# A routed layer's output rows: written with the residual on a token's first visit, added to on its second

## The chip, the cores and the metric

The kernel runs on one core of one Trainium2 chip. The metric is the device time of one execution in microseconds (us). Of the core's engines, TensorE (PE) multiplies, VectorE (DVE) and ScalarE (ACT) work on tiles, GpSimd (POOL) issues the transfers that go through lists of row numbers, and SyncE (SP) issues the other transfers; 16 DMA engines carry them out.

## The reference, cut to what matters

A decoder layer: attention and a recurrence make the residual stream `x`; then 1024 tokens go through a routed feed-forward block of 32 experts in 4 groups, each token to two experts of one group.

```python
h2 = rms_norm(x, norm2_g) * (1.0 + scale2) + shift2
x = x + gate2 * hierarchical_moe(h2, ...)
...
g_p, g_idx = lax.top_k(g_prob, 1)
e_p, e_idx = lax.top_k(jax.nn.softmax(e_logits, axis=-1), TOP_K)   # TOP_K = 2
expert = g_idx * EXPERTS_PER_GROUP + e_idx
...
hid = jax.nn.silu(xb @ w_gate[e]) * (xb @ w_up[e])
return hid @ w_down[e]
...
y = jnp.zeros((N + 1, D), jnp.float32).at[row_tok].add(y_rows)[:N]
```

## The kernel before, in words

The first 500 us compute the mixers and, tile by tile of 128 tokens, the residual row `x1`, its norm factor `ivx`, the router and the places of the tokens in their experts' lists. `h2_rows` writes each tile of `x1` to `out` (L1238, on POOL's queue) and `h2 = x1 * ivx` to `h2_d` in HBM (L1247, on SP's queue). `places` builds, by products of one-hot matrices, a table `tb` of token numbers and gate weights for all experts.

The experts then run as 20 units (`UNITS`). A unit is a block of 128 rows, filled by one expert or by up to four experts of different groups, in multiples of 32 rows. The two experts of a token never share a unit. Units 0 to 4 hold eight "front" experts (two of each group) whose weights are loaded early; the other 24 experts are ranked by their counts, and `overflow_tables` builds the lists of what runs over an expert's first 128 rows. For unit n:

- `gather` (L1437, POOL): an indirect DMA brings the unit's rows of `h2_d` into a buffer `xe`, of which there are `NXE` (two). A list entry outside the 1024 tokens is skipped.
- `xpose` (L1610, PE): eight transposes into `pxe`; ACT and DVE copy them out as `xeT` (L1614, L1616).
- `gate_up` (L1649, PE): products with the expert's gate and up weights into `pgu`; `act` (L1623, L1625) forms `hid`; `hid_t` (L1632, L1634) transposes it.
- `down` (L1660, PE): products with the down weights into `py`; DVE multiplies by the row `g2` into `y` (L1663); an indirect DMA adds the rows of `y` to the rows of `out` (L1665, POOL, a scatter).

The weights of an expert are six blocks of 512 KB, loaded by SP into the pool of 128x1024 blocks (`blk`, `NBLK` of them); a load waits for the fourth load before it (`fly`, L1125), so four are in flight. The loop calls `step` three times per unit; each takes one piece of `tables()` and puts it on DVE and PE between the unit's own work. A scheduler sets the final order on each engine. Transfers that touch the same tensor are ordered by semaphores: each scatter waits until the scatter before it has landed.

Of the kernel before, what the change touches and what calls it, by code (L numbers as in the profile page):

```python
# [20 lines left out]
D = 1024  # L21
S = 1024
# [20 lines left out]
ROWS = [("gqp", 64), ("gkp", 64), ("freq", 32), ("br", 36)]  # L43
# [52 lines left out]
MULTI = [u for u in UNITS if len(u) > 1]  # L96
NFU = 5
GRP = [("same", 32), ("in", 4), ("by", 4), ("base", 1), ("full", 32), ("shift", 32)]
GOFF = {}
_o = 0  # L100
for _n, _w in GRP:
# [37 lines left out]
def layer(ctx, tc, A, out, dbg=None, stop=None):  # L139
# [193 lines left out]
    V.tensor_scalar(tokm, tokc[:, :NT], -float(S), None, op0=OP.add)  # L333
# [840 lines left out]
    NXE = 2  # L1174
# [26 lines left out]
    rec = c2.tile([128, NT, 2, 2], F32, name="rec")  # L1201
    tb = c2.tile([128, 64], F32, name="tb")
# [32 lines left out]
    def h2_rows(t):  # L1235
        x1 = St[t]["x"]
        tsl = slice(t * 128, t * 128 + 128)
        G.dma_start(out[tsl, :], x1)  # L1238
        h2 = blk("h2")
        iv = ivx[:, t:t + 1]  # L1240
        if OPT["h2p"][t] == "S":
            SC.activation(h2, x1, AF.Copy, scale=iv)
        elif OPT["h2p"][t] == "V":
            V.tensor_scalar(h2, x1, iv, None, op0=OP.mult)
        else:
            G.tensor_mul(h2, x1, iv.to_broadcast([128, D]))
# [194 lines left out]
    def column(p, m):  # L1441
        if p < NF:
            e = FRONT[p]
            return tk0[:, e:e + 1], tb[:, 32 + e:33 + e]
        if m:
            c = EBASE[p] + m - 1
            return toi[:, c:c + 1], tow[:, c:c + 1]
        return tki[:, p:p + 1], tkw[:, p:p + 1]

    def plan(u):  # L1450
        if len(u) == 1:
            i, w = column(*u[0][:2])
        else:
            c = MULTI.index(u)
            i, w = pki[:, c:c + 1], pkw[:, c:c + 1]
        n = max(g[2] + g[3] for g in u) * 32
        return i[:n], w[:n], [(0, i[:n])]

    pki = c2.tile([128, len(MULTI)], I32, name="pki")
    pkw = c2.tile([128, len(MULTI)], F32, name="pkw")  # L1460
    xrow = {0: gather(plan(UNITS[0])[0])}

    def pack(pieces):
        for c, (p, m, a, n, r) in pieces:
            i, w = column(p, m)
            V.tensor_copy(pki[32 * a:32 * (a + n), c:c + 1], i[r:r + 32 * n])
            last["pack"] = V.tensor_copy(pkw[32 * a:32 * (a + n), c:c + 1], w[r:r + 32 * n]).ins

    def pieces(us, late):
        return [(MULTI.index(u), g) for u in us if len(u) > 1 for g in u if bool(g[1]) == late]  # L1470
# [30 lines left out]
    pT = bank("pT")  # L1501
    for c in range(2):
        T.transpose(pT[:32, c * 128:c * 128 + 128], tb[:, c * 32:c * 32 + 32], ident)
    tT = half("tT")[:32, :256]
    V.tensor_copy(tT, pT[:32, :256])
    pS_ = bank("psort")
    for c in range(2):
        T.matmul(pS_[:, c * 32:c * 32 + 32], tT[:, c * 128:c * 128 + 128], R, start=True, stop=True)
    tki = c2.tile([128, 32], I32, name="tki")
    V.tensor_scalar(tki, pS_[:, :32], trash, None, op0=OP.add)  # L1510
    tkw = c2.tile([128, 32], F32, name="tkw")
    V.tensor_copy(tkw, pS_[:, 32:64])
    tow = c2.tile([128, NOV], F32, name="tow")
    toi = c2.tile([128, NOV], I32, name="toi")
    pack(pieces(UNITS[2:NFU], False))
# [3 lines left out]
    def overflow_tables():  # L1519
# [47 lines left out]
        V.tensor_scalar(si, si, 7, None, op0=OP.logical_shift_right)  # L1567
# [4 lines left out]
        V.scalar_tensor_tensor(rec[:, :, :, 0], pf, -1.0, tokm[:, :, None].to_broadcast(SH), op0=OP.mult, op1=OP.add)  # L1572
        yield
        pto = bank("pto")[:, :2 * NOV]
        for c in range(2):
            for t0 in range(0, NT, 4):
                ts = slice(t0, t0 + 4)
                oh = t3(half("ov"), 4)
                V.tensor_tensor(oh, iota[:, None, :].to_broadcast([128, 4, 128]),
                                pf[:, ts, c:c + 1].to_broadcast([128, 4, 128]), op=OP.is_equal)  # L1580
                ob = half("ov")
                bo = t3(ob[:, 8 * NOV:12 * NOV], 4)
                V.tensor_tensor(bo, iota[:, None, :NOV].to_broadcast([128, 4, NOV]),
                                ext[:, ts, c:c + 1].to_broadcast([128, 4, NOV]), op=OP.is_equal)
                rh = ob[:, :8 * NOV].rearrange("p (t a e) -> p t a e", t=4, a=2)
                V.tensor_tensor(rh, bo[:, :, None, :].to_broadcast([128, 4, 2, NOV]),
                                rec[:, ts, c, :, None].to_broadcast([128, 4, 2, NOV]), op=OP.mult)
                for t in range(4):
                    T.matmul(pto, oh[:, t], rh[:, t].rearrange("p a e -> p (a e)"), start=(t0 + t == 0 and c == 0),
                             stop=(t0 + t == NT - 1 and c == 1))  # L1590
# [184 lines left out]
```

## Time and profile before

| | |
|---|---|
| median of 3 runs | 815.01 us (810.57 to 818.53) |
| the profiled execution | 816.49 us |
| its span, first to last instruction | 814.6 us |
| mean granted clock of PE | 0.971 of full |
| busy: PE, DVE, ACT, POOL | 728.1, 447.2, 317.0, 157.6 us |
| HBM read, written | 160.61 MB, 22.95 MB |

The span is some 500 us of mixers, norm and router, then the units. Busy times overlap; a share of the whole span hides that each stretch has a limit of its own. "Landing" of a transfer is the time from the start of the instruction that issues it until its data has arrived.

### The profile page before, as it was taken

Reading aid. Unit: us, or ns where it says so; the run is one execution under the profiler, and the core shown is the slowest. Engines: PE = TensorE matmul, PEld = TensorE weight load, DVE = VectorE, ACT = ScalarE, POOL = GpSimd, SP = SyncE. Lnnn points to the kernel's source line nnn. Section 1 sums busy time; section 2 is a strip of 40 time slices with the busy share of each in tenths; the row PEclk is TensorE's granted clock in tenths of the full one; section 3 lists DMA queues with packets and bytes.
Section 4 is the critical chain, followed back from the end, with each engine's and each line's share of the span. In section 5 each row is a group of like instructions: output and inputs, shape, how many; then the busy total and the mean of one; then the engine's idle time right before and its main releaser. Section 6 shows DMA issues by size and latency. Waiting matters only on the chain. (4 is left out here: it accounts for less than half of the span.)

```text
span 814.6 us, 12260 instructions
## 1 busy us (share of the span) xinstructions
PE 728.1 (89%) x4257; PEld 471.2 (58%) x4257; DVE 447.2 (55%) x1334; ACT 317.0 (39%) x715; POOL 157.6 (19%) x150
## 2 busy tenths in 40 slices
PE   3899999989988989899999997699979899999874
PEld 1477776548877878788888886333333343332321
DVE  4597386868777469797884667344334222213210
ACT  3455456666354157667664434121201211102200
POOL 1121012103665102031311000212112112212010
PEclk9989999999999999999999998699989999999998
DMA  9952437681317403020154789999999999999994
GB/s 311 372 151 84 143 108 236 210 280 58 109 44 259 168 39 104 1 79 1 54 173 144 259 311 343 346 316 349 313 373 330 329 335 336 369 347 354 304 320 102
DMA packets 70976, 180.47 MB, mean 222 GB/s; under 512 B 8960, under 2 KB 22528, under 8 KB 70912
## 3 DMA queue, kind: packets, MB, share of 16 engines
q1 hardware_dynamic: 63328, 158.50, 55.1%
q0 software_dynamic: 7104, 21.00, 9.5%
q8 instruction: 34, 0.56, 0.3%
q10 hardware_dynamic: 480, 0.16, 0.2%
q14 instruction: 30, 0.25, 0.1%
HBM read 160.61 MB, written 22.95 MB: 225 GB/s over the span
## 5 line engine op out<-in xcount | busy, mean ns | idle before, releaser
L1649 PE MATMUL pgu<-ew,xeT 128*32 128x512 f32 (+1 forms) x928 | 163.4, 613 | 8.1 <-DMA ew<-in_w_e 7.3
L1649 PEld LDWEIGHTS pgu<-ew,xeT 128*32 128x32 f32 (+1 forms) x928 | 48.3, 121 | 99.4 <-issue 79.0
L1660 PE MATMUL py<-ew,hT 128*32 128x512 f32 (+1 forms) x464 | 75.1, 597 | 5.8 <-ACT hT L1634 5.8
L225 PE MATMUL pp<-hTh,winh 128*128 128x512 f32 x176 | 69.2, 406 | 5.8 <-DVE hTh L188 3.0
L226 PE MATMUL pp<-hTl,winh 128*128 128x512 f32 x176 | 71.1, 404 | 0.0
L227 PE MATMUL pp<-hTh,winl 128*128 128x512 f32 x176 | 70.4, 401 | 0.0
L1663 DVE TENSOR_TENSOR y<-py,m_g 128x512 f32<-128x512 f32 (+1 forms) x40 | 27.5, 691 | 69.3 <-PE py L1660 64.3
L1623 ACT ACTIVATE sg<-pgu 128x256 f32<-128x256 f32 (+1 forms) x20 | 7.7, 387 | 142.9 <-PE pgu L1649 135.8
L1660 PEld LDWEIGHTS py<-ew,hT 128*32 128x32 f32 (+1 forms) x464 | 23.5, 120 | 48.3 <-issue 35.7
L1616 DVE TENSOR_SCALAR xeT<-pxe,gc,mc 128x128 f32<-128x128 f32 x80 | 27.4, 404 | 33.0 <-PE pxe L1610 33.0
L225 PEld LDWEIGHTS pp<-hTh,winh 128*128 128x128 f32 x176 | 34.0, 194 | 16.3 <-DVE hTh L188 4.0
L1665 POOL DMA_INDIRECT out<-y,pki x13 | 20.7, 1589 | 111.2 <-DVE y L1663 87.7
L1625 DVE SCALAR_TENSOR_TENSOR hid<-sg,pkw,pgu 128x256 f32<-128x256 f32 (+1 forms) x13 | 6.2, 479 | 63.4 <-ACT sg L1623 60.9
L1634 ACT ACTIVATE hT<-pht 128x256 f32<-128x256 f32 (+1 forms) x20 | 7.6, 380 | 85.1 <-PE pht L1632 65.4
L1614 ACT ACTIVATE xeT<-pxe,mc,gc 128x128 f32<-128x128 f32 x80 | 30.0, 461 | 24.9 <-PE pxe L1610 24.9
L226 PEld LDWEIGHTS pp<-hTl,winh 128*128 128x128 f32 x176 | 33.9, 193 | 9.9 <-issue 2.1
L227 PEld LDWEIGHTS pp<-hTh,winl 128*128 128x128 f32 x176 | 34.1, 194 | 8.6 <-issue 1.7
L949 ACT ACTIVATE P<-pS,nb,scq 128x384 f32<-128x384 f32 (+2 forms) x48 | 32.3, 679 | 12.2 <-DVE nb L946 12.2
L983 PE MATMUL po<-PT,v 128*128 128x256 f32 (+1 forms) x160 | 35.8, 362 | 0.0
L1046 POOL TENSOR_TENSOR wo<-wo,m_g 128x256 f32<-128x256 f32 x32 | 28.2, 916 | 15.3 <-DMA wo<-in_w_out 15.3
L983 PEld LDWEIGHTS po<-PT,v 128*128 128x128 f32 x160 | 28.8, 191 | 2.9
L1610 PEld LDWEIGHTS pxe<-ident,xe 128*128 128x128 f32 x160 | 18.2, 145 | 20.7 <-issue 14.4
(424 smaller groups left out, 1613.6 us busy)
## 6 DMA issues: line engine op xcount, KB each, us to landing
ew<-in_w_e SPq DMA_DIRECT2D x186, 512.0 KB
wad<-in_w_ada SPq DMA_DIRECT2D x64, 256.0 KB
wada<-in_w_ada SPq DMA_DIRECT2D x16, 512.0 KB
win<-in_w_in SPq DMA_DIRECT2D x12, 512.0 KB
xt<-in_x SPq DMA_DIRECT2D x8, 512.0 KB
wo<-in_w_out SPq DMA_DIRECT2D x8, 512.0 KB
xr<-in_x SPq DMA_DIRECT2D x8, 512.0 KB
x_d<-xr SPq DMA_DIRECT2D x8, 512.0 KB
```

Of the source, the lines that this page charges most:

```text
L225: T.matmul(o, lhi, rhi, start=first, stop=False)
L226: T.matmul(o, lhi, rlo, start=False, stop=False)
L227: T.matmul(o, llo, rhi, start=False, stop=last)
L949: SC.activation(Pt[:, o:o + w], pss[ci], AF.Exp, scale=P["scq"][:, i:i + 1], bias=nb, accum_out=l[:, ci:ci + 1])
L983: T.matmul(po[:, o:], P["v"][:, js], PT[j // 4][:, j % 4, o:], start=(j == 0), stop=(j == nj - 1), skip_group_check=True)
L1046: EN[OPT["g1"]].tensor_mul(w[:, q:q + 256], w[:, q:q + 256], mrow["g1"][:, q:q + 256])
L1614: SC.activation(xT[a][:, c], pt[:, c], AF.Identity, scale=gc[:, k:k + 1], bias=sh2[:, k:k + 1])
L1616: last["dve"] = V.tensor_scalar(xT[a][:, c], pt[:, c], gc[:, k:k + 1], sh2[:, k:k + 1], op0=OP.mult, op1=OP.add).ins
L1649: T.matmul(pg[r], xT[k // 4][:, c + r.start:c + r.stop], w[k // 2][:, NS[k % 2]], start=(k == 0), stop=(k == 7), skip_group_check=True)
L1660: T.matmul(py[n][r], hT[:, a * 128 + r.start:a * 128 + r.stop], w[4 + a][:, NS[n]], start=(a == 0), stop=(a == 1), skip_group_check=True)
L1663: last["dve"] = V.tensor_mul(y[:rows, NS[n]], py[n][:rows], mrow["g2"][:rows, NS[n]]).ins
L1665: G.indirect_dma_start(out=out, out_offset=bass.IndirectOffsetOnAxis(ap=idx, axis=0), in_=y[r0:r0 + idx.shape[0]], in_offset=None, compute ...
```

## The change

`h2_rows` no longer writes `x1` to `out`. The tables carry a third value per row: `1/ivx` where the row is the token's first visit in the order of the units, 0 where it is the second. `down` forms `x * r + y` in the gathered buffer (`x` is `h2`, so `h2/ivx = x1`) and sends it to `out` by two indirect DMAs in place of one: first the add, with the list of second visits, then a plain write, with the list of first visits; each list has an entry outside the tokens in the rows of the other. Unit 0 has no add. There are three `xe` buffers and 40 blocks. `tb` holds the front experts alone; the tables of all others are built by one pass (`late_tables`), of which a `step` takes three pieces.

```diff
-NBLK = 41
+NBLK = 40
-NX = 2
+NX = 3
...
+ONCE = {}
+for _n, _u in reversed(list(enumerate(UNITS))):
+    for _g in _u:
+        if _g[0] < NF:
+            ONCE[FRONT[_g[0]] // GE] = _g[0]
...
     def h2_rows(t):
...
-        G.dma_start(out[tsl, :], x1)
...
     def places(g):
...
+        inc = sm.tile([128, 2, 32], F32, name="inc", bufs=1)
+        V.tensor_tensor(inc, pp3, RW("cff")[:, None, :].to_broadcast([128, 2, 32]), op=OP.is_lt)
+        V.tensor_mul(scr, inc[:, :, None, :].to_broadcast([128, 2, 2, 32]), M[:, ts])
+        fst = two(2, "fst")
+        V.tensor_reduce(fst, scr, op=OP.add, axis=AX.X)
+        V.reciprocal(rinv[:, ts], ivx[:, ts])
+        V.tensor_mul(fst, fst, rinv[:, ts, None].to_broadcast([128, 2, 2]))
+        for c in range(2):
+            V.tensor_sub(rec[:, ts, c, 2], rinv[:, ts], fst[:, :, 1 - c])
...
+    def lists(c0, c1, src=None, dst=None):
+        v = pk[:, c0:c1] if src is None else src
+        get, put, add, t = dst or [x[:, c0:c1] for x in (idx["get"], idx["put"], idx["add"], fsh)]
+        V.tensor_scalar(get, v[:, :, 0], float(OOB), None, op0=OP.add)
+        V.tensor_scalar(t, v[:, :, 2], 0.0, 2.0 * OOB, op0=OP.is_gt, op1=OP.mult)
+        V.scalar_tensor_tensor(put, v[:, :, 0], 3.0 * OOB, t, op0=OP.add, op1=OP.subtract)
+        last["pack"] = V.scalar_tensor_tensor(add, v[:, :, 0], float(OOB), t, op0=OP.add, op1=OP.add).ins
+
+    def pack(c0, c1):
+        for c in range(c0, c1):
+            for p, m, a, n, r in UNITS[c]:
+                V.tensor_copy(pk[32 * a:32 * (a + n), c], source(p, m)[r:r + 32 * n])
+        lists(c0, c1)
+        done[0] = c1
...
-    def overflow_tables():
+    def late_tables():
...
+        for c in range(2):
+            V.tensor_tensor(bo[:, c], iota[:, None, :64].to_broadcast([128, NT, 64]),
+                            ext[:, :, c:c + 1].to_broadcast([128, NT, 64]), op=OP.is_equal)
+            yield
+            kt = t3(half("kt"), NT)
+            V.tensor_mul(kt, bo[:, c], uk[:, None, :].to_broadcast([128, NT, 64]))
+            V.tensor_reduce(key[:, :, c:c + 1], kt, op=OP.add, axis=AX.X)
+            yield
...
         for n in range(2):
-            last["dve"] = V.tensor_mul(y[:rows, NS[n]], py[n][:rows], mrow["g2"][:rows, NS[n]]).ins
-        for r0, idx in scat:
-            G.indirect_dma_start(out=out, out_offset=bass.IndirectOffsetOnAxis(ap=idx, axis=0),
-                                 in_=y[r0:r0 + idx.shape[0]], in_offset=None, compute_op=OP.add,
-                                 bounds_check=S - 1, oob_is_err=False)
+            V.tensor_mul(y[:rows, NS[n]], py[n][:rows], mrow["g2"][:rows, NS[n]])
+            last["dve"] = V.scalar_tensor_tensor(x[:rows, NS[n]], x[:rows, NS[n]], r, y[:rows, NS[n]],
+                                                 op0=OP.mult, op1=OP.add).ins
+        for ix, how in ((add, OP.add), (put, OP.bypass)):
+            if ix is not None:
+                G.indirect_dma_start(out=out, out_offset=bass.IndirectOffsetOnAxis(ap=ix, axis=0), in_=x[:rows],
+                                     in_offset=None, compute_op=how, bounds_check=S - 1, oob_is_err=False)
...
-                X[n + 1] = xpose(xrow.pop(n + 1))
-            step(1)
+                X[n + 1] = xpose(xrow[n + 1])
+            step(OPT["ls"])
...
-        down(u, hT, scat)
-        step(1)
+        down(u, hT, xrow.pop(n), (put, add if n else None, r))
+        step(OPT["ls"])
```

POOL's queue before, from the scatter of unit 0 on. `DMASW0` to `DMASW7` are completion semaphores that POOL's transfers take in turn: here gathers 0 to 4 have 0 to 4, scatter 0 has 5, gather 5 has 6, scatter 1 has 7, gather 6 has 0, scatter 2 has 1.

```order
L1665 DMA out_0<-y_5531,tk0_5370 1024x1024 [waits DMASW5_49,DMASW6_49,DVE_49,DMASW7_49,Activation_49,Pool_49]
L1437 DMA xe_5363<-h2_d_4041,pki_5376 128x1024 [waits DMASW3_49,PE_49]
L1665 DMA out_0<-y_5660,pki_5376 1024x1024 [waits DMASW5_49,DVE_49]
L1437 DMA xe_5362<-h2_d_4041,pki_5376 128x1024 [waits DMASW4_49,PE_49]
L1665 DMA out_0<-y_5809,pki_5376 1024x1024 [waits DMASW7_49,DVE_49]
```

A gather waits for the gather two before it, which had the same buffer, and for PE; a scatter waits for the scatter before it and for DVE.

The same queue after, from the gather of unit 2 on. Gathers 0 to 2 have `DMASW0` to `DMASW2`, the write of unit 0 has 3, gather 3 has 4, the add of unit 1 has 5, its write 6, gather 4 has 7, the add of unit 2 has 0, its write 1.

```order
L1459 DMA xe_5400<-h2_d_4041,idx_get_5412 128x1024 [waits DMASW2_49,DVE_49]
L1697 DMA out_0<-xe_5398,idx_put_5413 1024x1024 [waits DMASW3_49,DMASW0_49,DVE_49]
L1459 DMA xe_5398<-h2_d_4041,idx_get_5412 128x1024 [waits DMASW3_49,PE_49]
L1697 DMA out_0<-xe_5399,idx_add_5414 1024x1024 [waits DMASW1_49,DVE_49]
L1697 DMA out_0<-xe_5399,idx_put_5413 1024x1024 [waits DMASW5_49]
L1459 DMA xe_5399<-h2_d_4041,idx_get_5412 128x1024 [waits DMASW6_49,PE_49]
L1697 DMA out_0<-xe_5400,idx_add_5414 1024x1024 [waits DMASW2_49,DVE_49]
L1697 DMA out_0<-xe_5400,idx_put_5413 1024x1024 [waits DMASW0_49]
L1459 DMA xe_5400<-h2_d_4041,idx_get_5412 128x1024 [waits DMASW1_49,PE_49]
```

Between a unit's `y` and the gather three units on stand two transfers, each of which waits for the landing of the one before; the next unit's add stands behind that gather.

PE before, units 8 to 11: the first row transposes unit 11, the second is `gate_up` of units 9 and 10, then come the transposes of `hid` and `down` of unit 9, then `gate_up` of unit 11.

```order
L1610 MATMUL pxe<-ident,xe 128x128 x8
L1649 MATMUL pgu<-ew,xeT 128x512 x16
L1632 MATMUL pht<-ident,hid 128x128 x2
L1660 MATMUL py<-ew,hT 128x512
L1660 MATMUL py_6647<-ew,hT 128x512
L1660 MATMUL py<-ew,hT 128x512
L1660 MATMUL py_6647<-ew,hT 128x512
L1649 MATMUL pgu<-ew,xeT 32x512 x12
```

PE after, at the same place: `xpose` and `gate_up` of unit 10, `hid` and `down` of unit 9, `xpose` and most of `gate_up` of unit 11, `hid` of unit 10.

```order
L1638 MATMUL pxe<-ident,xe 128x128 x8
L1677 MATMUL pgu<-ew,xeT 128x512 x8
L1660 MATMUL pht<-ident,hid 128x128 x2
L1689 MATMUL py<-ew,hT 128x512
L1689 MATMUL py_6743<-ew,hT 128x512
L1689 MATMUL py<-ew,hT 128x512
L1689 MATMUL py_6743<-ew,hT 128x512
L1638 MATMUL pxe<-ident,xe 128x128 x8
L1677 MATMUL pgu<-ew,xeT 32x512 x24
L1660 MATMUL pht<-ident,hid 128x128 x2
```

The transposes of a unit now stand right ahead of its own `gate_up`, and `down` of the unit before stands behind that. From unit 3 on nearly every unit is in this order.

## Rows read from the trace of the kernel before

**Rows 1.** Busy time of each engine over the units, 541 to 806 us, with columns.
```profile
core 0: us, PE busy (x) PEld busy (x) DVE busy (x) ACT busy (x) POOL busy (x), PEclk, DMA share, GB/s
541.00:806.00 265.00, 241.85 (x1517) 87.90 (x1516) 73.59 (x203) 38.00 (x106) 45.85 (x34) 0.98 0.96 328
```

**Rows 2.** Waits of SP's queue, 400 to 814 us: total, times, longest.
```profile
SPq L1125 <- DMA ew<-in_w_e: 189.7, 151, 4.2
...
SPq L1125 <- PE pgu L1649: 13.2, 19, 2.9
```

**Rows 3.** Timeline of SP's queue, its last piece: start, us, instruction, count.
```profile
503.61 288.68 SPq L1125 DMA_DIRECT2D ew<-in_w_e  x156
```

**Rows 4.** Timeline of POOL, 471 to 807 us: start, us, instruction, idle before.
```profile
471.42 0.53 POOL L1238 DMA_DIRECT2D out<-xr  x1 [7.74 <-DVE xr L1214]
...
497.64 0.53 POOL L1238 DMA_DIRECT2D out<-xr  x1 [8.43 <-DVE xr L1214]
...
542.75 1.63 POOL L1665 DMA_INDIRECT out<-y,tk  x1 [7.59 <-ACT sg L1623]
...
671.96 1.57 POOL L1665 DMA_INDIRECT out<-y,tki  x1 [16.16 <-DVE y L1663]
676.33 1.05 POOL L1437 DMA_INDIRECT xe<-h_d,pki  x1 [2.80 <-PE pxe L1610]
683.46 1.58 POOL L1665 DMA_INDIRECT out<-y,toi  x1 [6.07 <-DMA out<-y,tki]
...
720.58 1.48 POOL L1665 DMA_INDIRECT out<-y,pki  x1 [0.30 <-issue]
...
806.85 1.55 POOL L1665 DMA_INDIRECT out<-y,pki  x1 [17.09 <-DVE y L1663]
```

**Rows 5.** Landing of the scatters, all that have one recorded.
```profile
DMA to landing us min/median/max: 6.3/9.4/10.7
```

**Rows 6.** Landing of the last scatter alone, 806 to 808 us.
```profile
DMA to landing us min/median/max: 6.3/6.3/6.3
```

**Rows 7.** Landing of the gathers, all that have one recorded.
```profile
DMA to landing us min/median/max: 7.7/8.0/9.9
```

**Rows 8.** Landing of the writes of `x1`, 512 KB each.
```profile
DMA to landing us min/median/max: 3.8/7.2/7.6
```

**Rows 9.** Timeline of all engines in unit 17, 760 to 775 us, cut to five rows.
```profile
760.55 1.09 PE L1610 MATMUL pxe<-ident,xe 128*128 128x128 f32 x8
...
761.58 7.05 PE L1649 MATMUL pgu<-ew,xeT 128*32 128x512 f32 x58
...
769.68 0.44 PE L1632 MATMUL pht<-ident,hid 128*128 128x128 f32 x2 [1.05 <-DVE hid L1625]
...
770.65 3.64 PE L1660 MATMUL py<-ew,hT 128*32 128x512 f32 x32 [0.53 <-ACT hT L1634]
...
773.53 1.52 DVE L1663 TENSOR_TENSOR y<-py,m_g 128x512 f32<-128x512 f32 x2 [2.62 <-PE py L1660]
```

**Rows 10.** Stretch behind PE's wait of some 4 us, by windows, columns as Rows 1.
```profile
788.00:791.00 3.00, 0.40 (x4) 0.16 (x8) 0.00 (x0) 0.00 (x0) 1.55 (x1) 1.00 0.96 355
791.00:795.00 4.00, 4.00 (x28) 1.10 (x24) 0.00 (x0) 0.00 (x0) 0.00 (x0) 0.57 0.96 264
```

**Rows 11.** Residual update of 128x512, by tile `xr`: min/median/max ns, first and last start.
```profile
L1214 DVE SCALAR_TENSOR_TENSOR xr<-pA,ivA,xr x16: 745/751/752, 429.6 to 496.6; 128x512 f32<-128x512 f32 x16
```

**Rows 12.** Timeline of DVE and PE from the router's end, 509 to 545 us.
```profile
509.78 0.22 DVE L1350 TENSOR_TENSOR tb<-tb,ptab 128x64 f32<-128x64 f32 x1 [2.12 <-PE ptab L1345]
510.04 0.24 DVE L1429 TENSOR_SCALAR tk<-tb,tokc 128x32 int32<-128x32 f32 x1
...
540.33 1.50 DVE L1663 TENSOR_TENSOR y<-py,m_g 128x512 f32<-128x512 f32 x2 [4.35 <-issue]
```

**Rows 13.** Groups of DVE instructions, 520 to 640 us: busy us, mean ns.
```profile
L1579 DVE TENSOR_TENSOR ov<-iota,pf 128x512 f32<-128x512 f32 x4 | 2.7, 682 | 0.0
...
L1557 DVE TENSOR_TENSOR mt<-M,fs 128x256 f32<-128x256 f32 x6 | 2.5, 418 | 0.0
```

More of the change, by code (lines that the diff above doesn't have):

```diff
@@ L58 @@
 EXTRA = {8: [128, 96], 9: [128, 32], 10: [64]}
-EBASE = {8: 1, 9: 4, 10: 7}
-NST = 8
+CB = {}
+NST = 0
+for _p in range(NF, 32):
+    assert _p not in EXTRA or CAP[_p] == 128
+    CB[_p] = NST
+    NST += 1 + len(EXTRA.get(_p, []))
 NOV = NST + 32
+OOB = 4096
 def slot_of(g, r):
@@ L1173, in layer @@
     sh2 = mc[1][:, 8:16]
-    NXE = 2
+    NXE = NX
     wrg = c2.tile([128, 8, 40], F32, name="wrg")
@@ L1439, in gather, with source @@
         return x
-    def column(p, m):
+    done = [0]
+    def source(p, m):
         if p < NF:
             e = FRONT[p]
[L1444 to L1470, printed above, removed]
@@ new lines, in pack, with plan @@
+    def pack(c0, c1):
[4 more added lines that the diff above has]
+        done[0] = c1
+    def plan(n):
+        rows = max(g[2] + g[3] for g in UNITS[n]) * 32
+        return [x[:rows, n:n + 1] for x in (idx["get"], idx["put"], idx["add"])] + [pk[:rows, n, v:v + 1] for v in (1, 2)]
+    pack(0, 1)
+    xrow = {0: gather(plan(0)[0])}
+    pack(1, 2)
+    xrow[1] = gather(plan(1)[0])
@@ L1499, in layer @@
     V.tensor_copy(permi, pP[0:1, :32])
[L1501 to L1515, printed above, removed]
+    pack(2, NFU)
+    late3 = t3(half("late")[:, :192], 3)
     nit = c2.tile([1, 1], I32, name="nit")
     item = c2.tile([1, 32], I32, name="item")
-    def overflow_tables():
+    uk = half("uk")[:, :64]
+    SC.dma_start(uk, bass.AP(tensor=A["ukey"].tensor, offset=A["ukey"].offset, ap=[[0, 128], [1, 64]]))
+    def late_tables():
         SH = [128, NT, 2]
@@ L1571, in overflow_tables @@
         V.scalar_tensor_tensor(pf, ext, -128.0, at, op0=OP.mult, op1=OP.add)
-        V.scalar_tensor_tensor(rec[:, :, :, 0], pf, -1.0, tokm[:, :, None].to_broadcast(SH), op0=OP.mult, op1=OP.add)
         yield
-        pto = bank("pto")[:, :2 * NOV]
+        bo = half("bo").bitcast(BF).rearrange("p (c t e) -> p c t e", c=2, t=NT)
+        key = full
         for c in range(2):
[L1576 to L1590, printed above, removed]
-                yield
@@ new lines, in late_tables, with products @@
+            yield
[4 more added lines that the diff above has]
+        for c in range(2):
+            V.tensor_tensor(more[:, :, c], key[:, :, c], key[:, :, 1 - c], op=OP.is_lt)
+        V.tensor_mul(rec[:, :, :, 2], more, rinv[:, :, None].to_broadcast(SH))
+        pto = bank("pto")[:, :192]
+        def products(c, t0, oh, rh):
+            for t in range(2):
+                T.matmul(pto, oh[:, t], rh[:, t].rearrange("p v e -> p (v e)"), start=(t0 + t == 0 and c == 0),
+                         stop=(t0 + t == NT - 1 and c == 1))
@@ L1604, in xpose @@
+        products(*ready)
+        V.tensor_copy(late3, t3(pto, 3))
+        pack(NFU, NFU + 4)
+        yield
+        for n in range(NFU + 4, len(UNITS), 4):
+            pack(n, min(n + 4, len(UNITS)))
+            yield
+    def tables():
+        yield from late_tables()
     def xpose(x):
@@ L1651, in gate_up, with down @@
         return pg
-    def down(u, hT, scat):
-        y = sm.tile([128, D], F32, name="y", bufs=2)
+    def down(u, hT, x, lists):
+        put, add, r = lists
+        y = sm.tile([128, D], F32, name="y", bufs=1)
         py = [bank("py"), bank("py1")]
@@ L1714, in layer @@
             u = [("late", 0, 0, 4, 0)]
-            hid = act(gate_up(u, xpose(gather(ixc))), wc)
-            down(u, hid_t(hid), [(0, ixc)])
+            x = gather(ixs[0])
+            hid = act(gate_up(u, xpose(x)), pc[:, 0, 1:2])
+            down(u, hid_t(hid), x, (ixs[1], ixs[2], pc[:, 0, 2:3]))
     stage.close()
```

99 lines of the change are left out of this document (56 added, 43 removed).

## The prediction

> **What bounds the kernel now.** I read the busy times by stretch first. From 541 to 806 us, while the units run, the DMA engines are busy 0.96 of the time and move 328 GB/s, and PE is busy 241.85 of 265 us [rows 1]: two resources near their end. Which of them the other waits for is read from SP's queue, where the weights are issued: 151 times a load waits for the load four before it, 189.7 us in all, and 19 times, 13.2 us in all, for PE to free a block [rows 2]. So the loads go at the pace of the DMA engines, 156 of them in 288.68 us, 1.85 us each [rows 3] with the gathers and scatters between them, and PE follows. The 20 units run from the scatter at 542.75 to the one at 806.85 [rows 4], (806.85 - 542.75) / 19 = 13.9 us a unit, of which PE's own work is 1.09 + 7.05 + 0.44 + 3.64 = 12.2 us [rows 9].
>
> The third view is POOL's timeline, and it is the one that matters here. A transfer from POOL takes long to land under this load: scatters 9.4 us in the median (the last one, on an empty machine, 6.3) [rows 5, 6], gathers 8.0 [rows 7]. Now this is hidden: a gather is issued two units ahead, and a scatter has the whole of the next unit to land. It shows where a scatter comes early: the one at 683.46 waited 6.07 us for the one issued at 671.96 [rows 4].
>
> **The change: the chain that it makes.** The orders of POOL show that a unit's write waits for the landing of its add, and the gather three units on, which takes the same buffer, for the landing of that write. The orders of PE show that the transposes of unit n+3 stand ahead of `down` of unit n+2. That closes a ring of two units. From `y` of unit n: add lands (A), write lands (B), gather lands (G), transposes 1.09, `gate_up` 7.05 with the 0.44 for `hid` in it, `down` of unit n+2 3.64 [rows 9], then `y` and the residual. The last is 1.52 [rows 9] and two updates of 128x512 at 0.75 [rows 11], 3.0 us. POOL needs 0.3 us from a release to its next issue [rows 4], three times. So two units take 12.2 + 3.0 + 0.9 = 16.1 us, and A + B + G.
>
> A + B: the trace has no scatter with half its rows left out, nor a plain indirect write. The lower end is the shortest scatter and the shortest write of `x1`, 6.3 + 3.8 = 10.1 [rows 6, 8]; the upper end is two loaded scatters, 18.8 [rows 5]. The rows of a unit are divided between the two, so I pay one loaded scatter, 9.4, and one that carries nothing: the write of 3.8 with a scatter's issue, 1.58, for its own 0.53 [rows 4, 8], 4.85. Sum 14.3. G: 8.0 [rows 7].
>
> PE now waits in every unit, which has a price of its own: after its wait of some 4 us near 788 the granted clock of the next 4 us was 0.57, mostly the lower of its two levels (1.2 GHz), which lost 4 x 0.43 = 1.7 us [rows 10]. Together 16.1 + 14.3 + 8.0 + 1.7 = 40.1 us for two units, **20.0 us a unit** against 13.9. POOL's own round (A + B, a gather's issue of 1.05 and three times 0.3, 16.3 us) is shorter and doesn't decide.
>
> Is the DMA still loaded at that pace? Of the 156 loads some 20 lie before 541 (37 us at 1.85). The other 136 need 252 us; 40 blocks hold six and a half experts, so the last are issued about unit 14, and units 2 to 14 at 20.0 us take 260 us. So it stays loaded, and the loaded landings hold, through unit 14. Behind that I take A + B = 6.3 + 4.85 = 11.2 and G = 6, between 3.8 and 8.0: 16.1 + 1.7 + 11.2 + 6 = 35.0, 17.5 us a unit.
>
> **The other parts.**
> - *The front.* Between the router and the first gather stand some eight more small DVE instructions at 0.22 to 0.24 us [rows 12]: +2 us. POOL's first gather and PE wait for them.
> - *The tables.* The late pass has two one-hots, two products and two sums of 512 columns (0.68 each) and sixteen halves (0.42 to 0.55) [rows 13] where there were twelve pieces worth 6 us: about 6 us more on DVE, in units 1 and 2. DVE is busy 73.59 of 265 us [rows 1], and in these units PE waits for the chain: taken at 0, and +6 at most once if `y` of unit 1 or 2 falls behind them.
> - *The writes of `x1`.* Eight transfers of 512 KB are gone; four of them lie at or after 471.42 [rows 4], where the loads compete. At a load's 1.85 us that would be 7.4 us, earned only while loads set the pace. In the forecast the chain does: 0.
> - *One block fewer, three buffers for two.* One load less ahead, 1.85 us at most, hidden under the chain. The third buffer lengthens the ring from n+2 to n+3 and is in the sum.
> - *19 more issues.* 19 x 1.58 = 30 us on POOL, busy 45.85 of 265 us [rows 1]; they are part of A and B.
> - *The end.* From the last `y`: 0.3 + 6.3 + 0.3 + 4.85 and the 1.45 us that now lie between the landing and the end of the span (814.6 - 806.85 - 6.3): 13.2 us.
>
> **The sum.** `y` of unit 0 ends at 541.8 [rows 12], with front and residual at 545.3. Its write lands after 0.3 + 9.4, gather 3 after 0.3 + 8.0, at 563.3; transposes 1.1, `down` of unit 1 3.6, `y` 3.0: unit 1 is done at 571. Then 13 units at 20.0 and 5 at 17.5: 571 + 260 + 87.5 = 918.5; with the end 931.7. The profiled execution had 1.9 us outside its span and stood 1.5 us above the median, so 931.7 + 1.9 - 1.5 = 932; I say **930 us**, 14% slower.
>
> **The rivals.**
> 1. *The chain holds, but lands lightly.* Each scatter has half the rows, and SP's loads can leave gaps. With A + B = 10.1, G = 4.3 (3.8 and half a microsecond more issue) and no clock loss: 16.1 + 14.4 = 30.5, 15.2 us a unit. 571 + 18 x 15.2 + 11 = 856, **857 us** against the median. Against it: half of the scatters take 9.4 us or more, and the 6.3 is the last one's, with no load beside it [rows 5, 6].
> 2. *The chain is hidden, the loads stay the bound (not slower).* It decides at POOL's landings: two units take 27.8 us now, so it needs A + B + G of at most 27.8 - 16.1 = 11.7 us. Then front and end cost 2 + 6.6 (14.7 from the last `y` with residual, for 8.1 now), the writes of `x1` give back up to 7.4, and the time is 816.5 + 8.6 - 7.4 - 1.5 = **816 us**, or a little under it where the residual rides for free. Against it: the three shortest landings of the trace, 6.3, 3.8 and 3.8, already make 13.9. The Trainium skill, DMA: Bandwidth & Descriptors, section Anatomy of one DMA — SWDGE (gpsimd) path, speaks for this rival: a transfer issued by GpSimd costs about 2.0 us fixed and its bytes at 436 GB/s. By it, as an estimate for some 420 KB a unit, A + B + G would be 12 us and a unit 14.1 us, no more than now. The trace doesn't agree: behind its issue of 1.55 us the last scatter took 4.7 us, with no load beside it, and the loaded ones nearly 8 [rows 4 to 6].
> 3. *The chain lands heavily.* A row left out costs as much as one that is sent, so A = B = 9.4, and G is the longest gather, 9.9 [rows 7]: 16.1 + 28.7 + 1.7 = 46.5, 23.2 us a unit; 571 + 418 + 17 = 1006, **1006 us**.
>
> **How the numbers follow.** Forecast 0.72, rival 1 0.15, rival 2 0.05, rival 3 0.08. The range takes in the forecast's own unknowns (A + B by 3 us, G by 2 us, the clock loss: some 2 us a unit, 40 us either way) and reaches towards rivals 1 and 3: 868 to 985. A measurement of this kernel tells about 1% from no change. Rival 2 alone could be within it or faster; I give 0.03 to no change, 0.02 to faster and 0.95 to slower.
>
> **What would show it.** In the changed kernel's trace: POOL's adds, writes and gathers released by DMA landings, not by DVE and PE; PE waiting for `xe` ahead of each unit's transposes for 5 us and more; units some 20 us apart; SP's loads waiting for PE's blocks more than for each other; the granted clock of the units below 0.98. I am wrong if a write is issued before its add has landed, if landings fall to 4 us, or if the last load still lands just ahead of the last unit.

## The result, and the profile after

| | before | after |
|---|---|---|
| median | 814.23 us of 4 runs (810.57 to 818.53) | 927.61 us of 4 runs (919.45 to 930.46) |
| the profiled execution, its span | 816.49, 814.6 us | 926.88, 925.0 us |
| mean granted clock of PE | 0.971 | 0.913 |
| busy: PE, DVE, ACT, POOL | 728.1, 447.2, 317.0, 157.6 us | 745.0, 484.7, 317.2, 173.2 us |
| HBM read, written | 160.61, 22.95 MB | 160.66, 28.59 MB |

The ratio is 1.137 (95% interval 1.128 to 1.147): 113 us slower, against a forecast of 930 us. PE has 17 us more of busy time, and the span is 110 us longer: the engines wait.

Busy time by windows in the kernel after, columns as in [rows 1]: four stretches, then all units.

```profile
600.00:650.00 50.00, 38.54 (x302) 11.75 (x294) 11.80 (x22) 4.70 (x13) 8.28 (x7) 0.89 0.88 318
650.00:700.00 50.00, 28.94 (x164) 10.86 (x164) 9.10 (x18) 4.32 (x12) 9.94 (x8) 0.79 0.98 359
700.00:750.00 50.00, 39.70 (x150) 16.91 (x150) 13.47 (x27) 6.48 (x18) 8.33 (x7) 0.90 0.52 171
...
850.00:916.00 66.00, 48.38 (x288) 17.87 (x288) 19.64 (x36) 7.25 (x20) 14.08 (x11) 0.91 0.24 47
545.00:916.00 371.00, 259.01 (x1512) 97.86 (x1510) 107.08 (x255) 37.90 (x105) 68.18 (x55) 0.85 0.69 235
```

PE was busy 241.85 of 265 us at a granted clock of 0.98, the DMA 0.96 [rows 1]. Now PE is busy 259 of 371 us at 0.85, and the DMA 0.69. Over the whole of the units no resource is full any more (the DMA still is from 650 to 700 us, at 0.98), which is the look of a chain of waits. The added HBM writes of the table aren't rows sent: POOL's DMA queue moved 21.00 MB before and 16.82 MB after. Who waits, PE first, then POOL, 505 to 925 us (total, times, longest):

```profile
PE pxe L1638 <- DMA xe<-h_d,idx_get: 102.0, 14, 15.5
```
```profile
POOL out L1697 <- DVE xe L1693: 124.9, 13, 31.0
POOL out L1697 <- DMA out<-xe,idx_add: 112.3, 19, 9.5
...
POOL xe L1459 <- DMA out<-xe,idx_put: 50.6, 11, 7.9
```

PE stands 102 us ahead of the transposes for a gather that hasn't landed. POOL stands for the landing of each of the 19 adds ahead of its write, and for that of a write ahead of a gather. SP's queue, the waits in the same stretch and the last piece of its timeline:

```profile
SPq L1139 <- DMA ew<-in_w_e: 135.9, 122, 3.9
SPq L1139 <- PE pgu L1677: 82.7, 25, 30.4
...
SPq L1139 <- PE py L1689: 32.8, 9, 19.6
```
```profile
504.11 341.48 SPq L1139 DMA_DIRECT2D ew<-in_w_e  x156
```

The 156 loads took 288.68 us and waited 13.2 us for blocks that PE still held [rows 2, 3]; they now take 341.48 us and wait 82.7 + 32.8 = 115.5 us for PE.

One ring, from the add of unit 5 to that of unit 7: POOL's timeline (start, us, instruction, idle before).

```profile
654.11 1.60 POOL L1697 DMA_INDIRECT out<-xe,idx_add  x1 [0.30 <-issue]
662.75 1.01 POOL L1697 DMA_INDIRECT out<-xe,idx_put  x1 [7.04 <-DMA out<-xe,idx_add]
670.26 1.04 POOL L1459 DMA_INDIRECT xe<-h_d,idx_get  x1 [6.50 <-PE pgu L1677]
678.11 1.60 POOL L1697 DMA_INDIRECT out<-xe,idx_add  x1 [6.81 <-DVE xe L1693]
...
695.16 1.59 POOL L1697 DMA_INDIRECT out<-xe,idx_add  x1 [0.52 <-DVE xe L1693]
```

And PE's behind that gather:

```profile
678.73 1.50 PE L1638 MATMUL pxe<-ident,xe 128*128 128x128 f32 x8 [2.95 <-DMA xe<-h_d,idx_get]
680.02 8.43 PE L1677 MATMUL pgu<-ew,xeT 128*128 128x512 f32 x16
...
689.14 3.64 PE L1689 MATMUL py<-ew,hT 128*32 128x512 f32 x32 [0.47 <-ACT hT L1662]
```

The add of unit 5 lands after 8.4 us and the write starts 0.24 us later; the write lands after 6.7 and the gather of unit 8 starts 0.8 us later; the gather lands after 8.4, at 678.66, and the transposes start at 678.73. Transposes and `gate_up` of unit 8 and then `down` of unit 7 end at 692.8, the residual of unit 7 at 694.9, and the add of unit 7 follows: 41.05 us for two units. Every link starts within 1 us of the end of the one before it. (The gather's wait is put down to PE's `pgu`, since that came last by the records; the write had landed 0.8 us earlier, and so it is in each of the rings 1 to 14, by 0.74 to 0.84 us.)

### The profile page after: what moved, and what is told of

Read it like the earlier page. It is cut to its first block, busy times and chain, and to the rows that moved or that the text cites. A ratio compares the mean times of both kernels' runs of the same rounds, so it can differ in the third digit from the quotient of the medians.

```text
span 925.0 us, 12376 instructions
## 1 busy us (share of the span) xinstructions
PE 745.0 (81%) x4251; PEld 481.0 (52%) x4251; DVE 484.7 (52%) x1420; ACT 317.2 (34%) x715; POOL 173.2 (19%) x162
## 3 DMA queue, kind: packets, MB, share of 16 engines
q0 software_dynamic: 8656, 16.82, 6.9%
HBM read 160.66 MB, written 28.59 MB: 205 GB/s over the span
## 5 line engine op out<-in xcount | busy, mean ns | idle before, releaser
L1677 PE MATMUL pgu<-ew,xeT 128*32 128x512 f32 (+1 forms) x928 | 170.7, 654 | 0.8 <-ACT xeT L1642 0.7
L1638 PE MATMUL pxe<-ident,xe 128*128 128x128 f32 x160 | 31.5, 359 | 102.0 <-DMA xe<-h_d,idx_get 102.0
L1677 PEld LDWEIGHTS pgu<-ew,xeT 128*32 128x32 f32 (+1 forms) x928 | 50.7, 131 | 97.5 <-issue 80.3
L1638 PEld LDWEIGHTS pxe<-ident,xe 128*128 128x128 f32 x160 | 25.0, 185 | 117.0 <-DMA xe<-h_d,idx_get 114.2
L1689 PE MATMUL py<-ew,hT 128*32 128x512 f32 (+1 forms) x464 | 77.3, 604 | 3.4 <-ACT hT L1662 3.4
L1697 POOL DMA_INDIRECT out<-xe,idx_add x19 | 30.6, 1611 | 111.4 <-DVE xe L1693 93.9
L1459 POOL DMA_INDIRECT xe<-h_d,idx_get x20 | 20.7, 1036 | 148.5 <-DVE cnt L1502 66.9
L1697 POOL DMA_INDIRECT out<-xe,idx_put x20 | 21.0, 1050 | 143.4 <-DMA out<-xe,idx_add 112.3
L1060 POOL TENSOR_TENSOR wo<-wo,m_g 128x256 f32<-128x256 f32 x32 | 27.7, 898 | 17.2 <-DMA wo<-in_w_out 17.2
```

Source lines behind the costliest of these rows:

```text
L1060: EN[OPT["g1"]].tensor_mul(w[:, q:q + 256], w[:, q:q + 256], mrow["g1"][:, q:q + 256])
L1638: T.transpose(pt[:, b * 128:(b + 1) * 128], x[:, k * 128:(k + 1) * 128], ident)
L1677: T.matmul(pg[r], xT[k // 4][:, c + r.start:c + r.stop], w[k // 2][:, NS[k % 2]], start=(k == 0), stop=(k == 7), skip_group_check=True)
L1689: T.matmul(py[n][q], hT[:, a * 128 + q.start:a * 128 + q.stop], w[4 + a][:, NS[n]], start=(a == 0), stop=(a == 1), skip_group_check=True)
L1697: G.indirect_dma_start(out=out, out_offset=bass.IndirectOffsetOnAxis(ap=ix, axis=0), in_=x[:rows], in_offset=None, compute_op=how, bounds_ ...
```

## The experiments

The kernel before ran beside each group of runs (medians of 811.9 to 815.8 us), and ratios are to it.

### What the chain costs, and what the rest of the change

**Only the tables and the late pass.** The `x1` writes are back, one scatter-add of `y` per unit, two `xe` buffers, two `y` tiles, 40 blocks.

```diff
+        G.dma_start(out[tsl, :], x1)
...
-            V.tensor_mul(y[:rows, NS[n]], py[n][:rows], mrow["g2"][:rows, NS[n]])
-            last["dve"] = V.scalar_tensor_tensor(x[:rows, NS[n]], x[:rows, NS[n]], r, y[:rows, NS[n]],
-                                                 op0=OP.mult, op1=OP.add).ins
+            last["dve"] = V.tensor_mul(y[:rows, NS[n]], py[n][:rows], mrow["g2"][:rows, NS[n]]).ins
-        for ix, how in ((add, OP.add), (put, OP.bypass)):
+        for ix, how in ((add, OP.add),):
```

> The new tables, the late pass and 40 blocks stay; the residual is written tile by tile as before, and a unit has one scatter that adds y, with two gather buffers. Theory of the ring: the tables and the front cost 2 to 6 us, 816 to 822 us. Rival, the added DVE work of the tables and the later lists: 840 us or more.

817.21 us (814.48 to 820.97), ratio 1.004 (1.001 to 1.006), as expected: the front, the tables and the block less cost some 3 us together. The other 110 us come with what this kernel lacks: the residual in the unit, and two transfers out of the gathered buffer.

**The kernel before without the writes of `x1`.**

```diff
-        G.dma_start(out[tsl, :], x1)
```

> The kernel before without the eight writes of x1 to the output (the residual is left out). This is the most that the change could take off while the loads set the pace: 7.4 us by four transfers at a load's 1.85 us, 806 to 811 us. Rival: the loads wait for the norm and router there and nothing is earned, 812 to 815 us.

811.85 us against 811.89, ratio 0.999 (0.997 to 1.002): the eight writes that the change removes were worth nothing even where the loads set the pace, so what I expected first, 806 to 811 us, was a miss.

### What the two landings are made of

**The write goes to another tensor,** so it doesn't wait for the add.

```diff
+    first_d = dram.tile([S, D], F32, name="first_d")
...
-                G.indirect_dma_start(out=out, out_offset=bass.IndirectOffsetOnAxis(ap=ix, axis=0), in_=x[:rows],
+                G.indirect_dma_start(out=out if how == OP.add else first_d, out_offset=bass.IndirectOffsetOnAxis(ap=ix, axis=0), in_=x[:rows],
```

> The write of the first visits goes to another tensor in HBM, so that it doesn't wait for the landing of the add; the output then holds second visits alone. Both transfers stay, and the gather still waits for both. Theory of the ring: one landing of some 5 us, less an issue of 1.6 us, leaves the ring of two units, some 2 us a unit: about 890 us (880 to 905). Rival, the added work: 920 to 930 us.

891.68 us (888.61 to 893.47), ratio 1.093 (1.088 to 1.098), as expected. POOL's timeline of this kernel:

```profile
667.84 1.60 POOL L1698 DMA_INDIRECT out<-xe,idx_add  x1 [11.58 <-DVE xe L1694]
669.75 1.04 POOL L1698 DMA_INDIRECT first_d<-xe,idx_put  x1 [0.31 <-issue]
678.62 1.53 POOL L1460 DMA_INDIRECT xe<-h_d,idx_get  x1 [7.83 <-DMA first_d<-xe,idx_put]
```

The write is issued 0.31 us behind the add, and the gather then waits once, for the later of the two. One landing of two is out of the ring, and 36 of the 113 us are back.

**All rows in the add, none in the write.** Both transfers are issued as before, but every entry of the write's list is outside the tokens.

```diff
-        V.scalar_tensor_tensor(put, v[:, :, 0], 3.0 * OOB, t, op0=OP.add, op1=OP.subtract)
+        V.scalar_tensor_tensor(put, v[:, :, 0], 3.0 * OOB, t, op0=OP.add, op1=OP.max)
-        last["pack"] = V.scalar_tensor_tensor(add, v[:, :, 0], float(OOB), t, op0=OP.add, op1=OP.add).ins
+        last["pack"] = V.tensor_scalar(add, v[:, :, 0], float(OOB), None, op0=OP.add).ins
```

> The changed kernel with all rows of a unit in the add's list and none in the write's (from unit 1 on; the output isn't the layer's, since the first rows are added to what is there). The order of waits stays. If the rows of a unit are paid once and an empty write has its fixed price, as the sum had it, A + B stays what it is: 915 to 940 us, with the write landing in 2 to 4 us and the add in 8 to 9. Rival, a row left out costs as much as one that is sent: the write lands in 5 to 7 us, and the time is 950 us or more.

925.39 us (924.47 to 928.88), ratio 1.139 (1.135 to 1.143), the same as the change and as expected. Its POOL timeline:

```profile
650.99 1.60 POOL L1697 DMA_INDIRECT out<-xe,idx_add  x1 [0.30 <-issue]
661.38 1.01 POOL L1697 DMA_INDIRECT out<-xe,idx_put  x1 [8.80 <-DMA out<-xe,idx_add]
667.08 1.04 POOL L1459 DMA_INDIRECT xe<-h_d,idx_get  x1 [4.69 <-DMA out<-xe,idx_put]
```

The full add takes 10 us and the write of nothing still 5. Over units 1 to 14 the adds land after 9.05 us in the mean (6.0 to 10.3) and the empty writes after 4.1 (2.1 to 6.9): 13.1, where the change has 7.55 + 5.35 = 12.9. The rows are paid once, wherever they stand, and the second transfer costs its 4 us even with no row in it. The single writes are less clear than their mean: six landed after 2.1 to 2.7 us, as expected, and eight after 4.9 to 6.9 us, about the rival's 5 to 7. The time alone doesn't settle it, since it would stay the same too if a row left out cost as much as one sent. What speaks against that rival is that the landings move with the rows: from the change to this kernel the add takes 1.5 us more and the write 1.25 less. That rows left out carry nothing also stands in POOL's DMA queue (packets, MB, share), first of the change, then of the zeros-first kernel further down, which has one scatter per unit:

```profile
q0 software_dynamic: 8656, 16.82, 6.9%
```
```profile
q0 software_dynamic: 5952, 16.80, 8.4%
```

The 19 more transfers are 2704 more packets, and 0.02 MB.

### Breaking the ring

**The result in a tile of its own.** `x * r + y` goes to `y`, so that `xe` is free when DVE has read it; two `y` tiles, and a block less for the room.

```diff
-NBLK = 40
+NBLK = 39
-        y = sm.tile([128, D], F32, name="y", bufs=1)
+        y = sm.tile([128, D], F32, name="y", bufs=2)
-            last["dve"] = V.scalar_tensor_tensor(x[:rows, NS[n]], x[:rows, NS[n]], r, y[:rows, NS[n]],
+            last["dve"] = V.scalar_tensor_tensor(y[:rows, NS[n]], x[:rows, NS[n]], r, y[:rows, NS[n]],
...
-                G.indirect_dma_start(out=out, out_offset=bass.IndirectOffsetOnAxis(ap=ix, axis=0), in_=x[:rows],
+                G.indirect_dma_start(out=out, out_offset=bass.IndirectOffsetOnAxis(ap=ix, axis=0), in_=y[:rows],
```

> The result of a unit goes into the tile y (two of them, 39 blocks) and is sent from there, so that a gather no longer waits for the landing of a write out of its buffer. Same transfers, same work. Theory of the ring: the gather's landing leaves the ring, what stays is POOL's round of add, write and one gather's issue, some 15 us a unit: about 850 us (835 to 870). Rival, the added work itself (19 more indirect transfers, residual updates, tables): no change, 920 to 930 us.

841.29 us (837.23 to 846.46), ratio 1.032 (1.025 to 1.039). As expected, this one edit takes 86 us of the 113 away: same transfers and same residual, but a gather no longer waits for landings out of its own buffer. PE's waits for `xe` fall from 102.0 us to this:

```profile
PE pxe L1638 <- DMA xe<-h_d,idx_get: 21.0, 9, 6.9
```

The order on POOL changed with it: from unit 4 on a gather stands ahead of the write in nearly every unit.

```profile
640.26 1.59 POOL L1697 DMA_INDIRECT out<-y,idx_add  x1 [9.26 <-DVE xeT L1644]
643.40 1.05 POOL L1459 DMA_INDIRECT xe<-h_d,idx_get  x1 [1.55 <-issue]
647.28 1.01 POOL L1697 DMA_INDIRECT out<-y,idx_put  x1 [2.83 <-DMA out<-y,idx_add]
654.94 1.62 POOL L1697 DMA_INDIRECT out<-y,idx_add  x1 [6.65 <-DMA out<-y,idx_put]
```

The write still waits for its add, and the next add for that write: POOL's round, 14.7 us here (forecast 16.3). The adds of units 5 to 14 stand (777.82 - 640.26) / 9 = 15.3 us apart.

**Four `xe` buffers** instead, the result still in `xe`, 39 blocks.

```diff
-NX = 3
+NX = 4
```

> Four gather buffers (39 blocks) in place of three, nothing else: the gather three units on finds its buffer free one unit earlier. Theory of the ring: as with an own result tile, POOL's round of some 15 us a unit is left, about 850 us (835 to 870). Rival, the added work: 920 to 930 us. Rival, too few weight blocks: slower than 928 us, since there is one block fewer.

849.13 us (841.69 to 851.26), ratio 1.040 (1.033 to 1.047), as expected. The ring now spans three units, and a third of its 40 us is 13.3. The adds of units 1 to 15 are 16.05 us apart, though ((786.19 - 561.43) / 14), the pace of POOL's round: from 647.08 to 662.40 us an add of 7.9 us and a write of 6.4 stand one behind the other.

Both leave some 25 to 35 us. What follows asks for these.

**Own tile, and the write elsewhere:** the first and the third of the edits above together, 39 blocks.

> Both waits are cut: the result has a tile of its own, and the write of first visits goes to another tensor in HBM, so that adds wait for adds alone (the output holds second visits alone). Theory of the ring: POOL's round of two landings, which is all that the kernel with an own tile has left over the one before, goes too; the loads set the pace again at some 13.9 us a unit: 815 to 825 us. Rival, the work of two transfers a unit: 835 us or more, as with the own tile.

846.36 us (842.94 to 850.14), ratio 1.042 (1.038 to 1.046): a miss. I had held POOL's round of two landings, which stands in the timeline of the own-tile kernel, to be what is left. It is gone here (POOL waits 0.3 us for landings in all) and nothing is earned:

```profile
POOL out L1698 <- DVE y L1694: 207.7, 18, 21.1
```
```profile
PE pxe L1639 <- DMA xe<-h_d,idx_get: 26.8, 8, 7.3
```

PE waits for gathers as before. There was a second limit of about the same length right behind the first.

**Zeros first, then one scatter-add of `x * r + y`.** SP writes zeros to `out` early on, the list of all rows is added from `y`, there is no second transfer; three `xe`, 39 blocks.

```diff
+    for t in range(NT):
+        SY.dma_start(out[t * 128:(t + 1) * 128, :], xe[2])
...
-        for ix, how in ((add, OP.add), (put, OP.bypass)):
+        for ix, how in ((add, OP.add),):
```

> A version without the ring: zeros are written to the output at about 310 us, where the DMA engines have little to do, and each unit has one scatter that adds x * r + y from its own tile. The writes of x1 are gone from the busy stretch, and no landing stands in a ring. It keeps the new tables (3 us by the run with these alone) and the residual's 1.5 us behind the last unit, and gives back up to 7.4 us: 810 to 819 us.

837.82 us (833.39 to 843.84), ratio 1.030 (1.026 to 1.034): a miss again. Its POOL timeline (this execution took 843.84 us):

```profile
592.92 1.58 POOL L1700 DMA_INDIRECT out<-y,idx_get  x1 [16.87 <-DVE y L1696]
594.80 1.04 POOL L1462 DMA_INDIRECT xe<-h_d,idx_get  x1 [0.31 <-PE pgu L1680]
603.16 1.58 POOL L1700 DMA_INDIRECT out<-y,idx_get  x1 [7.32 <-DVE y L1696]
...
622.85 1.59 POOL L1700 DMA_INDIRECT out<-y,idx_get  x1 [16.75 <-DVE y L1696]
```

The gather comes right behind the scatter, since the residual reads `xe` at the very end of its unit. So a ring of two units is left, without A and B but with G: from 592.92 to 622.85, 30 us for two units where 27.8 are to be had (units 1 to 15 are 15.0 us apart, (782.35 - 572.70) / 14). The residual itself, read from the gathered buffer, holds that buffer.

**The same with four `xe` buffers,** 38 blocks.

```diff
-NBLK = 39
+NBLK = 38
-NX = 3
+NX = 4
```

> Zeros first, one scatter a unit from its own tile, and now four gather buffers (38 blocks) in place of three. What theory e8's miss leaves: a gather can't start until the residual of the unit three before it is read, at that unit's end, so that one landing of 8 us still stands in the ring of two units; a fourth buffer takes it out. Then 812 to 820 us. Rival, what is lost in e8 is the work of the residual and the tables or the blocks given up: 835 us or more, since the work is the same and there is one block fewer.

829.28 us (825.99 to 831.80), ratio 1.017 (1.013 to 1.021). The fourth buffer earns some 10 us, a miss: the time lies between the 812 to 820 us expected and the rival's 835. PE's waits for `xe` fall to 13.2 us, but not to none.

**The own tile with four `xe` buffers,** both landings on POOL, 38 blocks.

> The changed kernel with the result in its own tile and four gather buffers (38 blocks): neither the writes' landings nor the held buffer stand in PE's ring any more; the add still waits for the write before it, and the write for its add. If POOL's round of two landings and a gather's issue, some 15 us, is then the limit: 835 to 850 us. If the held buffer was all that was left in e1 and e5: 815 to 825 us.

843.58 us (841.75 to 845.97), ratio 1.036 (1.031 to 1.041), as expected. Here POOL's own round is the limit: its waits from 541 us on, and DVE's, which can't write `y` before the tile's last write has landed:

```profile
POOL out L1697 <- DMA out<-y,idx_put: 79.9, 15, 8.7
POOL out L1697 <- DMA out<-y,idx_add: 65.9, 15, 8.3
```
```profile
DVE y L1692 <- DMA out<-y,idx_put: 61.4, 8, 11.0
```

So either of the two limits alone, the gathers or the landings on POOL, holds the kernel near 840 us, and the kernel that lifts both comes to 829. That one has a transfer less in each unit as well; own tile, write elsewhere and four buffers together weren't run, so what the second transfer costs by itself isn't parted there. With three buffers it was some 10 us (ratio 1.042 with the write elsewhere, 1.030 with zeros first).

**Two controls: the tables alone with 38 blocks, and zeros first with four buffers and no residual.** The first edit is against the tables-alone kernel, the second against zeros first with four buffers.

```diff
-NBLK = 40
+NBLK = 38
```

> The kernel with only the tables and the late pass, but 38 blocks where it had 40: nothing else differs, and it computes the whole reference. It asks what the two blocks given up for a fourth gather buffer and a second result tile cost the zeros-first kernel, whose loads end at the same time but whose last units come some 8 us later. If the blocks cost it: 826 to 832 us, 1.5 to 2% above the kernel before. If they don't, because what bounds this end of the program is the speed of the loads and not how far ahead they stand: 815 to 820 us, and the 12 us of the zeros-first kernel lie in the residual or in the four buffers' gathers.

```diff
-            V.tensor_mul(y[:rows, NS[n]], py[n][:rows], mrow["g2"][:rows, NS[n]])
-            last["dve"] = V.scalar_tensor_tensor(y[:rows, NS[n]], x[:rows, NS[n]], r, y[:rows, NS[n]],
-                                                 op0=OP.mult, op1=OP.add).ins
+            last["dve"] = V.tensor_mul(y[:rows, NS[n]], py[n][:rows], mrow["g2"][:rows, NS[n]]).ins
```

> Zeros first, four gather buffers, own result tile, one scatter-add, 38 blocks as before, but without the VectorE operation that adds x times r to y: the output lacks the residual. A gather then no longer waits for the end of the unit that held its buffer. If the residual (1.5 to 3 us of VectorE between the down product and the scatter, and the buffer held until then) is what keeps the zeros-first kernel behind: 815 to 820 us, about that of the tables with 38 blocks in the same call. If the residual costs nothing once four buffers stand: 826 to 831 us, as with it; then the zeroed rows or the order of the gathers are left.

820.89 us (817.36 to 825.84), ratio 1.009 (1.006 to 1.011), and 818.46 us (813.78 to 822.79), ratio 1.005 (1.003 to 1.008). Two blocks fewer cost some 4 us; the residual costs some 10 us (829.28 to 818.46). POOL's timeline without the residual:

```profile
618.26 1.59 POOL L1698 DMA_INDIRECT out<-y,idx_get  x1 [6.85 <-DMA out<-y,idx_get]
622.66 1.04 POOL L1462 DMA_INDIRECT xe<-h_d,idx_get  x1 [2.81 <-PE pxe L1641]
628.32 1.59 POOL L1698 DMA_INDIRECT out<-y,idx_get  x1 [4.61 <-DVE y L1695]
```

A gather is now released by the transposes (`pxe`), not by the end of a unit. PE's waits for `xe` fall with it from 13.2 to 3.0 us, which points to this hold; but the two updates of DVE ahead of each scatter go too, and no run parts them, so it stays open. None of the twelve kernels beats the kernel before. The nearest that still does the residual in the unit is zeros first with four buffers, 1.7% slower.

## Why the prediction was right, and where only by luck

**The ring** was right in its links and in its length. Units 1 to 15 are 20.06 us apart ((855.94 - 575.07) / 14), forecast 20.0. Rings 1 to 13, each from its add to the add two units on, take 39.9 us in the mean, forecast 40.1; they divide as follows.

| | forecast | measured, mean of 13 |
|---|---|---|
| A + B | 14.3 | 7.55 + 5.35 = 12.9 |
| G | 8.0 | 6.85 |
| POOL's releases after A and B | 0.6 | 0.27 + 0.79 |
| from the gather's landing to `y` with its residual: PE, DVE, clock | 12.2 + 3.0 + 1.7 = 16.9 | 17.3 |
| from `y` to its add | 0.3 | 1.75 |

Landings were 2.6 us too long in the forecast, the rest 2.3 too short: errors of opposite sign, so that 40.1 lies so near to 39.9 by luck. Landing times of all adds, writes and gathers in 570 to 850 us, in this order (min, median, max):

```profile
DMA to landing us min/median/max: 4.5/7.6/10.8
DMA to landing us min/median/max: 2.5/5.4/7.9
DMA to landing us min/median/max: 3.8/7.6/9.4
```

The price of A + B, one loaded scatter for all the rows and one empty transfer, was the choice between ends of 10.1 and 18.8, and the kernel with all rows in the add shows it as such: 9.05 for the first (forecast 9.4) and 4.1 for the empty one (4.85).

**The release of the add** was the term put too low, 0.3 us for 1.75. The change section has it that the next unit's add stands behind the gather; the sum gave that no time. In four of the 13 rings (adds of units 5, 10, 12 and 14) the result had been ready for 3.2 to 7.5 us, while POOL stood at that gather, which waited for the write before it to land. Unit 12, on DVE and then on POOL:

```profile
783.96 0.75 DVE L1693 SCALAR_TENSOR_TENSOR xe<-xe,pk,y 128x512 f32<-128x512 f32 x1
```
```profile
790.82 1.04 POOL L1459 DMA_INDIRECT xe<-h_d,idx_get  x1 [6.61 <-DMA out<-xe,idx_put]
792.16 1.60 POOL L1697 DMA_INDIRECT out<-xe,idx_add  x1 [0.30 <-issue]
```

**The clock loss** came out near its size, though from a thin base. I took 1.7 us from one wait of 4 us; waits are up to 15.5 us long now, and the clock of the units is 0.85, not 0.98. In the ring above eight transposes take 1.50 us for 1.09 [rows 9] and `gate_up` 8.43, where the same form took 7.03 in the kernel before: 1.8 us more. Over all units PE's busy time grew by 259.01 - 241.85 = 17.2 us, 0.9 a unit.

```profile
639.20 7.03 PE L1649 MATMUL pgu<-ew,xeT 128*128 128x512 f32 x16
```

**"It stays loaded, and the loaded landings hold, through unit 14"** failed in its first half. SP waited up to 30.4 us for blocks of PE, and from 700 to 750 us the DMA share was 0.52; the gathers of 706 to 765 us landed after 3.8 to 4.5 us. Four of the thirteen rings had them, and landings of 4 us were one of the signs of being wrong. The loads did last until unit 14 or so (504.11 + 341.48 = 845.6; its add is at 831.68), by the waits for PE. What I gave as its sign, that loads wait for PE more than for each other, isn't there either: 115.5 against 135.9 us. Nor are the adds released by landings: 14 of 19 waited for DVE. The other signs are there, the waits for `xe` by 14 records.

**The last units** were too dear: the five from unit 14 on take 914.39 - 831.68 = 82.7 us, forecast 87.5. The first of them takes 24.3, the other four 14.6 each ((914.39 - 855.94) / 4). Landings of adds, writes and gathers behind 850 us, in this order:

```profile
DMA to landing us min/median/max: 5.9/6.1/6.2
DMA to landing us min/median/max: 2.1/2.5/2.9
DMA to landing us min/median/max: 4.2/4.3/4.3
```

A + B is 8.6, not 11.2: I had built the write that carries nothing from the shortest write of `x1`, 512 KB in 3.8 us [rows 8], and the writes of the last units take 2.5. G is 4.3, not 6.

**The front and the sum.** The add of unit 1 stands at 575.07, forecast 571.3: write 0 at 547.95 (545.6), the gather behind it landed in 9.1, and transposes and `down` at a lower clock, 1.97 + 4.56 us for 1.09 + 3.64. Against the forecast span of 931.7 the start is 3.8 later, units 2 to 14 are 3.4 shorter, the last five 4.8, and the end, from 0.3 us ahead of the last add, 2.3 (10.9 for 13.2): 931.7 + 3.8 - 3.4 - 4.8 - 2.3 = 925.0.

**The small parts.** 0 for the `x1` writes holds, and more strictly than argued: they are worth 0 even without the chain. The tables at 0 hold within the 3 us of the tables-alone kernel.

**The rivals.** Light landings (857) failed by 12.9 + 6.85 against its 10.1 + 4.3. The hidden chain (816) needed A + B + G of 11.7 us; it is 19.8. It also fails without load: behind 850 us, at a DMA share of 0.24, the sum is 12.9. The rule of the Trainium skill that spoke for it, DMA: Bandwidth & Descriptors, section Anatomy of one DMA — SWDGE (gpsimd) path, gives, as an estimate, 3.2 us for 512 KB by its 2.0 us and the bytes. Behind 850 us the gathers come near that if their issue is taken off (4.3 - 1.04 = 3.3), the adds don't (6.1 - 1.6 = 4.5), and under the loads neither does (7.6 us each with their issue). The prediction's 12 us by it come out only with the three issues on top; the rule alone would make A + B + G some 8 us, as an estimate. Heavy landings (1006) failed since an empty transfer costs 4, not 9.

**What the 113 us are made of**, by the runs: about 3 the tables; 86 the landings in the ring of the gathers (own tile); the other 24 stand behind two limits side by side, POOL's two landings per unit and the gather that waits for the residual. Lifting one of them earned nothing; the kernel that lifts both, with one transfer per unit and two blocks given up for the room, earned some 12. It is still some 14 behind the kernel before, of which the residual is some 10.

## What to carry to other kernels

A buffer that is filled by one transfer and sent out by another puts the landings of both into the loop that reuses it; send the result from a tile of its own, or count the landings as if they were compute (here 20 us in 40). Two transfers to the same tensor, each with half the rows, aren't two halves: the rows are paid once, but the second pays its landing, rows or no rows. Where a ring is broken and a part of the loss remains, look for a second wait of the same length right behind the first, and lift both in one kernel before judging either.

## What the runs showed of the hardware

An indirect write whose every row is left out still took 2.1 us on a quiet machine and up to 6.9 us under the loads to land. An add of all rows landed after 9.05 us in the mean, one of the second visits alone after 7.55: by these two, the number of rows is the smaller part of it. The eight 512 KB writes from POOL, four of them between 471 and 500 us among the loads, were free to within 0.3%.
